# Moving one modulation vector from the value products to the first feed-forward block, with its steps ordered behind block products

## The chip, the cores and the metric

The kernel runs on one core of one Trainium2 chip, as one program. The core has a matrix engine (TensorE, PE in the profile, with its weight loads as PEld), VectorE (DVE), ScalarE (ACT), GpSimd (POOL) and a queue engine (SyncE, SP) that issues most of the transfers. Each engine works through its own list of instructions in order, and waits at the head of that list. The metric is the device time of one execution in microseconds (us), given as the median of several runs.

## The reference

Two layers of a diffusion backbone work on 512 latent and 256 context tokens of width 1024, all in float32. Every sub-layer normalises its input, scales and shifts it by a modulation vector, and adds its result to the stream through a gated post-norm. Layer 0 mixes tokens by gated linear attention and by softmax attention. Layer 1 mixes by a gated recurrence (HGRN2). Each is followed by a SwiGLU feed-forward block (FFN, 2816 hidden columns).

```python
m_lat = jnp.split((sc @ mod_w[l] + mod_b[l])[:, None, :], 6, axis=-1)
h_lat = _modulate(_rms(x_lat, norm_pre_mix[l]), m_lat[0], m_lat[1])
...
x_lat = x_lat + m_lat[2] * _rms(o_lat @ w_out, norm_post_mix[l])
h_lat = _modulate(_rms(x_lat, norm_pre_ffn[l]), m_lat[3], m_lat[4])
x_lat = x_lat + m_lat[5] * _rms(_swiglu(h_lat, ffn_w_gate[l], ffn_w_up[l], ffn_w_down[l]), norm_post_ffn[l])
```

There are thus six modulation vectors per layer, each a product of an activated condition (1024) with a block of `mod_w` of 1024 by 1024, 4 MB. The context tokens have six more from the same weights. In layer 1 the context is not needed behind the mixer, so only the vectors 0 and 1 are computed for it there. The text below writes (l, m) for vector m of layer l. The vector (1,4) scales the input of the second FFN; it is needed after layer 1's mixer.

## The kernel before

**Products.** Every float32 product is made as three products of split operands. ScalarE rounds an operand to its high part (wH, x, b11 and others), VectorE subtracts that to get the low part (wL and others), and `mm3` multiplies high by high, high by low and low by high. All matmuls are recorded at line 355 and all transposes at line 358, so tile names tell them apart.

**Modulation vectors.** `mod_late` (line 560) makes a vector without TensorE until its end. For each of eight blocks of 128 rows it loads 512 KB (line 578, on SP's queue) into a ring of two buffers (`mraw`), and VectorE multiplies the block by one number per partition and adds it to a sum (`macc`, lines 594 and 596). At the end TensorE adds the sum over the partitions (`mod_acc`), VectorE copies the row (line 469), TensorE transposes it (`modT`), and VectorE adds the bias (line 481). Where a gate follows, `gate_rows` (line 637) multiplies by a gain, transposes (`gcT`) and stores the row in HBM; `gate_row` (line 658) later loads it to all partitions as `gv`. `mod_late` is a generator: each call makes one step or a few, and hands back control. A call loads the next block before it sums the present one.

**The first FFN** (`ffn`, line 1544). `first` (line 1581) makes the first four columns of blocks and sums of the normalised input, split at line 98. Then for `idx` from 1 to 10 the gate and the up products are made by `seven` (line 839): seven block products in place of eight, each of 12 matmuls, into banks named a, E, b and D. VectorE and ScalarE add the banks to the outputs (lines 861 to 879) as each product ends. The weights come through `pair_operands` (line 801, with the splits of lines 798 and 799 and the sums of line 823). `seven` calls `fill` twice, behind its second and its fifth product, and `fill` calls the modulation generator `late` once. Before, `late` makes three jobs: (0,5) for both streams, (1,1) for both streams, and (1,5). `per=2` lets a job of one vector make two sums per call. At `idx` 9 whatever is left of `late` is issued at once, since its buffers are wanted.

**The down product** (`down`, line 1660) has seven passes over seven groups of blocks, with operands split at lines 1709 to 1712. Post-norms of finished tiles (`post_norm`, line 712; `pre_norm`, line 678) are generators in a list, and `tick` advances the earliest by one step. `turn` and `turn_next` issue the transposes of a tile (hT) whose normalised rows xn (line 685) are ready.

**The value products** stand at the end of the first FFN, in `values` (line 1997): the value columns of layer 1 for six tiles of tokens, in two halves c of 512 columns, with two tiles taken as a pair in each half. A tile and half has 24 matmuls (`nat`). Between tiles a generator `mods` makes vectors; before, its jobs are (1,2) together with (1,3), and then (1,4). The rest is drained when the products have been issued. Then `odd_mixer` (layer 1) begins with the products `ff` of its first head.

**What sets the order.** A planner puts each engine's instructions in a list before the run. It follows the order of the text where it must and takes ready work early where it may. While `self.pinned` is true, `pin` keeps TensorE's instructions in the order of the text; layer 1's mixer and the down products are pinned, the block products and, before, the value products are not. `tc.issue_after(ins)` makes every instruction issued inside it on `ins`'s engine follow `ins` in that engine's list; other engines and queues are not bound by it.

Of the kernel before, what the change touches and what calls it, by code (L numbers as in the profile page):

```python
# [8 lines left out]
F32 = mybir.dt.float32  # L9
# [4 lines left out]
ALU = mybir.AluOpType  # L14
# [50 lines left out]
class Forms:  # L65
# [29 lines left out]
    def split(self, n, f, i, m):  # L95
        H, L = (x[:, :, i : i + m] for x in self.tiles[n])
        self.net.nc.scalar.copy(H, f)
        self.net.nc.vector.tensor_tensor(L, f, H.bitcast(F32), op=ALU.subtract)

    def put(self, j, t):  # L100

# [215 lines left out]
class Net:  # L317
# [239 lines left out]
                yield  # L557
                rows()

    def mod_late(self, pool, jobs, tag="mraw", bufs=2, spare=None, per=1):  # L560


        nc = self.nc
        deep = bufs + (spare is not None) - 1
        for l, ms, then in jobs:
            self.mod_tiles(l, [m for m, r in ms if r == 0])
            accs = [pool.tile([P, D], F32, tag="macc", bufs=2, name=f"macc{l}{m}{r}") for m, r in ms]
            steps = [(k, m) for k in range(KD) for m in sorted({m for m, _ in ms})]
            us = []

            def load():
                i = len(us)
                k, m = steps[i]
                if spare is not None and i % (deep + 1) == deep:
                    u = spare()
                else:
                    u = self.wp.tile([P, WU], F32, tag=tag, bufs=bufs, name=f"mraw{l}{m}{k}")
                self.nc.sync.dma_start(out=u, in_=self.I["mod_w"][l, k * P : (k + 1) * P, m * D : (m + 1) * D])
                us.append(u)

            for _ in range(deep):
                load()
            yield
            done = 0
            for i, (k, m) in enumerate(steps):
                if len(us) < len(steps):
                    load()
                u, us[i] = us[i], None
                for a, (mm, r) in zip(accs, ms):
                    if mm != m:  # L590
                        continue
                    w = self.scT[:, k, r : r + 1]
                    if k == 0:
                        nc.vector.tensor_scalar(a, u, w, None, op0=ALU.mult)
                    else:
                        nc.vector.scalar_tensor_tensor(a, u, w, a, op0=ALU.mult, op1=ALU.add)  # L596
                    done += 1
                u = None
                if done % per == 0:
                    yield  # L600

            acc = self.tr_tile("mod_acc")
            for j in range(4):
                self.mm(
                    acc[32 * j : 32 * j + 32, :],
                    self.one.to_broadcast([P, 32]),
                    accs[(j // 2) % len(accs)][:, (j % 2) * 512 : (j % 2) * 512 + 512],
                    start=True,
                    stop=True,
                    tile_position=(0, 32 * j),  # L610
                )
            turned = self.mod_cols(l, acc, 512, [(m, r, 0, 2 * n, 0, 2) for n, (m, r) in enumerate(ms)])
            yield
            turned()
            if then:
                rows = self.gate_rows(l, *then)
                yield
                rows()
# [59 lines left out]
    def pre_norm(self, pool, t, xt, A, B, h):  # L678

        nc = self.nc  # L680
        r = 0 if t < LT else 1
        xn = pool.tile([P, D], F32, tag="xn", bufs=2, name=f"xn{t}")
        rs = self.rstd(self.sumsq(xt, xn), D)
        yield
        nc.vector.tensor_scalar(xn, xt, rs, None, op0=ALU.mult)
        tok = slice(t * P, (t + 1) * P)

        def turn():
            for hf in range(2):
                pt = self.tr_tile(f"hT{t}{hf}")  # L690
                forms = isinstance(h, Forms)
                f = h.at(hf, t) if forms else pool.tile([P, 4, P], F32, tag="hf", bufs=2, name=f"hf{t}{hf}")
                for kk in range(4):
                    k = hf * 4 + kk
                    self.tr(pt[:, kk * P : (kk + 1) * P], xn[:, k * P : (k + 1) * P], self.ident)
                for kk in range(4):
                    k = hf * 4 + kk
                    src = pt[:, kk * P : (kk + 1) * P]
                    nc.scalar.activation(f[:, kk, :], src, AF.Identity, bias=B[:, r, k : k + 1], scale=A[:, r, k : k + 1])
                if forms:  # L700
                    h.put(hf, t)
                else:
                    self.put(h, slice(hf * 4, hf * 4 + 4), tok, f)

        self.turns.append(turn)
# [133 lines left out]
    def seven(self, W, h, X, fill, then=None, turned=False):  # L839
# [4 lines left out]
        for wn, hn, x in SEVEN:  # L844
# [21 lines left out]
                        then()  # L866
                fill()
            elif wn == "12":
                nc.vector.tensor_tensor(c11, c11, pt, op=ALU.add)
            elif wn == "U2":  # L870
                nc.scalar.copy(c12, pt)
            elif wn == "22":
# [3 lines left out]
                nc.vector.tensor_tensor(c12, c12, pt, op=ALU.add)  # L876
            else:
                nc.vector.tensor_tensor(c21, c21, pt, op=ALU.subtract)
                nc.vector.scalar_tensor_tensor(c22, pt, -1.0, c22, op0=ALU.mult, op1=ALU.subtract)

    def rows_unit(self, w, c, pool=None):
        return self.unit(w[c * P : (c + 1) * P, :].rearrange("p (o n) -> p o n", o=1), 1, D, pool)
# [661 lines left out]
    def ffn(self, l, xp, yp, fp, pp, rp, h, ending, extra=None):  # L1544
# [5 lines left out]
        np_ = NFC // 2  # L1550
        self.blocks = I["ffn_w_down"][l].rearrange("(i k p) m -> k p i m", k=2, p=P)
        extra = extra or iter(())
        fill = lambda: next(extra, None)
        self.banks(True)
        qp = self.open_pool(f"q{l}", "right")
        qa = qp.tile([P, np_, 2, n], F32, name="qa")
# [60 lines left out]
        for idx in range(1, np_):  # L1617
            c0 = 2 * idx
            if qb[idx] is None:
                for _ in extra:  # L1620
                    pass
                qb[idx] = fp.tile([P, D], F32, tag="macc", bufs=2, name="qb")[:, : 2 * n].rearrange("p (a b) -> p a b", a=2)
            step = fill if idx > 1 else lambda: None
            last = []
            if idx == np_ - 1:
                down = self.down(l, fp, qp, rp, xp, quad, early, tiles, n, ending, lambda: todo())
# [33 lines left out]
    def down(self, l, fp, qp, rp, xp, quad, early, tiles, n, ending, finish):  # L1660
# [93 lines left out]
        for p, (name, where) in enumerate(seven):  # L1754
# [4 lines left out]
            for at, (g, i) in enumerate(order):  # L1759
# [43 lines left out]
                elif name == "22":  # L1803
                    plus(y1[:, low], b)
                    self.later(end(y1, t1))
                    self.tick()
                    if l and i == nh - 1:
                        close = final(dp, y0, t0)
                else:
# [8 lines left out]
    def run(self):  # L1818
# [162 lines left out]
        for _ in mods:  # L1981
            pass
        h1 = Split(ha)
        late = self.mod_late(
            fp, ((0, ((5, 0), (5, 1)), (5, R_NQF)), (1, ((1, 0), (1, 1)), None), (1, ((5, 0),), (5, R_NQF, 1))), per=2
        )

        def ending(dp):
# [8 lines left out]
            def values():  # L1997
# [1 line left out]
                self.tr_tile("pre"), self.sc_tile("pre", 0), self.sc_tile("pre", 1)  # L1999
                fi = yp.tile([P, len(order), D], F32, tag="y", bufs=1, name="fi")  # L2000
                spare = lambda: fp.tile([P, 2, 2 * forms.n], F32, tag="go", bufs=1, name="mraw").rearrange("p a n -> p (a n)")[:, :WU]
                mods = self.mod_late(fp, ((1, ((2, 0), (3, 0)), (2, R_NQM, 1)), (1, ((4, 0),), None)), spare=spare)
                for c in range(2):
                    pairs = [order[4:], order[:2]][c]
                    for t in order:
# [4 lines left out]
                        for i in range(4):  # L2010
                            W = value(c, i)
                            for a, x in enumerate(ts):
                                for k in (2 * i, 2 * i + 1):
# [4 lines left out]
                                        k == 0,  # L2018
                                        k == KD - 1,
                                    )  # L2020
                            if len(ts) > 1 and c == 0:
                                next(mods, None)
                                value(1, i)
                            if len(ts) > 1 and c == 1:
                                next(mods, None)
                        for a, x in enumerate(ts):
                            self.nc.scalar.copy(fi[:, x, 512 * c : 512 * c + 512], pt[:, 512 * a : 512 * a + 512])
                        if c == 0 and len(ts) == 1:
                            self.turn_next()
                            self.tick(5)  # L2030
                        if len(ts) == 1 and (c or t == order[3]):
                            for _ in range(4):
                                next(mods, None)
                for _ in mods:
                    pass
                ep.release()
# [109 lines left out]
```

## Time and profile before

| | |
|---|---|
| median of 3 runs | 1719.78 us (1719.2 to 1720.59) |
| the profiled execution | 1718.21 us, span 1716.3 us |
| busy: TensorE, weight loads | 1649.0 us, 1479.8 us |
| busy: VectorE, ScalarE, GpSimd | 1313.2 us, 929.7 us, 131.0 us |
| granted TensorE clock, mean | 0.991 |
| moved by DMA | 204.79 MB, mean 119 GB/s |

The stages around the change, from the timeline: the first FFN's entry from about 418 us, its block products from 457 to 754 us, its down product to 921 us, the value products to 999 us, then layer 1's mixer.

A row of the timeline gives start, length, engine, line, operation, output and inputs with their shapes, how often, and in brackets how long the engine sat idle before it and what ended that. A row of waits gives who waited for whom: total us, times, longest. A row of windows gives a stretch, its length, each engine's busy time with the count of instructions, the granted clock and the share of the DMA engines. A row of the chain gives start, length and what the chain that ended last was doing. Matmuls overlap, so starts tell more than lengths.

### The profile page before, as it was taken

What the parts mean: (1) busy time and instruction counts of PE and PEld (TensorE: products, weight loads), DVE (VectorE), ACT (ScalarE), POOL (GpSimd) and SP (SyncE); (2) the same over time, 40 slices, a digit from 0 to 9 for tenths busy, and PEclk for the clock granted to TensorE, in tenths of its full rate; (3) what the DMA queues carried; (4) which work ended last, traced back from release to release, by engine and by line L of the source; (5) the groups of instructions that cost most, each with busy time, mean ns of one, the idle gap of its engine ahead of it and who ended that gap; (6) DMA issues with size and microseconds to landing.
All of it is one profiled execution on the core that took longest, in us unless ns stands there. A gap on an engine that the chain in (4) does not pass through costs nothing.

```text
span 1716.3 us, 32583 instructions
## 1 busy us (share of the span) xinstructions
PE 1649.0 (96%) x13359; PEld 1479.8 (86%) x13359; DVE 1313.2 (77%) x2138; ACT 929.7 (54%) x1615; POOL 131.0 (8%) x135
## 2 busy tenths in 40 slices
PE   6999998999999999999998969999999999999997
PEld 5899987888999999998876758888988899999875
DVE  4889678875987898677667547878775489998887
ACT  4745568846544444445457316666564465555654
POOL 1004110011000000003101000000000000000221
PEclk9999999999999999999999979999999999999999
DMA  9641012175332435249426642112115333433793
GB/s 324 190 151 40 2 49 86 48 234 169 91 92 72 135 111 160 68 159 193 79 94 237 196 135 75 47 43 63 50 28 171 112 121 111 123 100 92 194 193 135
DMA packets 184961, 204.79 MB, mean 119 GB/s; under 512 B 7366, under 2 KB 142060, under 8 KB 184812
## 3 DMA queue, kind: packets, MB, share of 16 engines
q1 hardware_dynamic: 173760, 181.82, 33.7%
q0 software_dynamic: 9120, 17.30, 5.8%
q10 hardware_dynamic: 1932, 3.59, 0.6%
q8 instruction: 104, 1.70, 0.4%
q14 instruction: 45, 0.37, 0.1%
HBM read 193.23 MB, written 9.46 MB: 118 GB/s over the span
## 4 chain that ended last, share of the span: by engine, by line
PE 79%; DVE 8%; DMA 6%; ACT 4%; issue 2%; POOL 0%; SPq 0%; DVEq 0%; POOLq 0%; ACTq 0%
PE a L355 11%; PE nat L355 10%; PE ff L355 8%; PE x L355 8%; PE E L355 7%; PE oproj L355 5%; PE o L355 4%; PE D L355 4%; PE b L355 4%; DMA mraw<-in_mod_w_dram 3%; PE fq L355 3%; PE gqk L355 2%; PE q L355 2%; PE S L355 1%; PE poh L355 1%
## 5 line engine op out<-in xcount | busy, mean ns | idle before, releaser
L355 PE MATMUL nat<-wH,x 128*128 128x256 f32 (+2 forms) x992 | 232.8, 324 | 7.2 <-ACT x L709 3.3
L355 PEld LDWEIGHTS nat<-wH,x 128*128 128x128 f32 x992 | 167.3, 191 | 26.6 <-ACT x L709 4.8
L798 ACT CAST wH<-raw 128x1024 fp32r<-128x1024 f32 x120 | 125.5, 1051 | 107.2 <-PE b L355 29.8
L799 DVE TENSOR_TENSOR wL<-raw,wH 128x1024 fp32r<-128x1024 f32 x120 | 146.1, 1221 | 37.1 <-ACT wH L798 36.5
L355 PE MATMUL nat<-wL,x 128*128 128x256 f32 (+2 forms) x496 | 158.8, 320 | 0.4 <-DVE wL L744 0.3
L743 ACT CAST wH<-raw 128x1024 fp32r<-128x1024 f32 (+1 forms) x84 | 85.9, 1036 | 94.3 <-PE ff L355 34.1
L744 DVE TENSOR_TENSOR wL<-raw,wH 128x1024 fp32r<-128x1024 f32 (+1 forms) x84 | 99.9, 1199 | 48.1 <-ACT wH L743 47.3
L667 POOL TENSOR_TENSOR rs<-ms,neghalf 128x1 f32<-128x1 f32 (+2 forms) x62 | 69.9, 1131 | 861.0 <-DVE ms L665 860.8
L355 PE MATMUL ff<-x,wH 128*128 128x512 f32 (+1 forms) x512 | 129.7, 344 | 0.0
L355 PE MATMUL x<-wH,two 128*128 128x512 f32 x310 | 102.4, 397 | 5.2 <-DVE two L1712 3.3
L355 PE MATMUL oproj<-wH,x 128*128 128x512 f32 x320 | 102.2, 395 | 0.4 <-ACT x L1262 0.4
L355 PEld LDWEIGHTS nat<-wL,x 128*128 128x128 f32 x496 | 94.7, 191 | 7.0 <-DVE wL L744 1.0
L596 DVE SCALAR_TENSOR_TENSOR macc<-mraw,scT,macc 128x1024 f32<-128x1024 f32 x70 | 89.1, 1279 | 14.0 <-DMA mraw<-in_mod_w_dram 13.8
L355 PEld LDWEIGHTS ff<-x,wH 128*128 128x128 f32 x512 | 89.1, 194 | 10.0
L1677 POOL DMA_DIRECT2D t<-in_ffn_w_down_dram x42 | 45.0, 1149 | 647.9 <-DVE wL L1711 619.6
L950 ACT COPY qkh<-arr 128x512 f32<-128x512 f32 x112 | 70.0, 641 | 36.3 <-DVE arr L955 32.2
L355 PE MATMUL ff<-x,wL 128*128 128x256 f32 (+1 forms) x256 | 87.1, 340 | 0.0
L823 DVE TENSOR_TENSOR raw<-raw 128x512 f32<-128x512 f32 x120 | 82.6, 688 | 2.3
L355 PEld LDWEIGHTS x<-wH,two 128*128 128x128 f32 x310 | 58.0, 189 | 20.5 <-DVE two L1712 6.5
L955 DVE TENSOR_TENSOR arr<-arr,f 128x512 f32<-128x512 f32 x112 | 74.2, 687 | 1.9 <-ACT qkh L950 0.3
L355 PE MATMUL a<-T,wH 128*128 128x384 f32 (+1 forms) x320 | 70.7, 310 | 0.3 <-ACT qb L861 0.2
L355 PE MATMUL E<-x,wH 128*128 128x384 f32 (+1 forms) x320 | 70.7, 310 | 0.0
(413 smaller groups left out, 4528.5 us busy)
## 6 DMA issues: line engine op xcount, KB each, us to landing
mraw<-in_mod_w_dram SPq DMA_DIRECT2D x80, 512.0 KB, 4.6
raw<-in_ffn_w_gate_dram SPq DMA_DIRECT2D x44, 512.0 KB, 4.2
raw<-in_ffn_w_up_dram SPq DMA_DIRECT2D x44, 512.0 KB, 3.8
raw<-in_odd_w_in_dram SPq DMA_DIRECT2D x40, 512.0 KB, 3.7
t<-in_ffn_w_down_dram POOLq DMA_DIRECT2D x24, 512.0 KB, 7.9
raw<-in_ffn_w_down_dram SPq DMA_DIRECT2D x22, 512.0 KB, 5.0
mraw<-in_mod_w_dram SPq DMA_DIRECT2D x32, 256.0 KB, 6.1
raw<-in_even_w_in_dram SPq DMA_DIRECT2D x16, 512.0 KB, 4.8
```

The costliest lines, as they stand in the source:

```text
L355: return self.pin(self.nc.tensor.matmul(*a, **k))
L596: nc.vector.scalar_tensor_tensor(a, u, w, a, op0=ALU.mult, op1=ALU.add)
L667: nc.gpsimd.tensor_tensor(rs, ms, self.neghalf.to_broadcast([P, w]), op=ALU.pow)
L743: nc.scalar.copy(H[:, :m], raw[:, :m])
L744: nc.vector.tensor_tensor(L[:, :m], raw[:, :m], H[:, :m].bitcast(F32), op=ALU.subtract)
L798: self.nc.scalar.copy(H, f)
L799: self.nc.vector.tensor_tensor(L, f, H.bitcast(F32), op=ALU.subtract)
L823: add = lambda o, x, y: nc.vector.tensor_tensor(o, x, y, op=ALU.add)
L950: nc.scalar.copy(qkv[:, :, :, half, :], dst)
L955: nc.vector.tensor_tensor(dst, dst, tb, op=ALU.mult)
L1677: add = lambda o, src: self.pin(nc.gpsimd.dma_start(out=o, in_=src, accum_op=ALU.add))
```

## The change

1. `late` in the first FFN gets a fourth job, (1,4). A job with two sums per block still makes one block per call; a job of one vector now makes three sums per call, not two (`per` becomes a function of the number of sums).
2. `seven`, `pre_norm` and `Forms.split` record some of their VectorE instructions in `self.mark`. `fill` issues the modulation steps under `issue_after(self.mark)`, so on VectorE they come behind the last recorded instruction. `fill` is now also called at `idx` 1.
3. In the value products `mods` keeps only (1,2) with (1,3). Its calls go through `mod`, which uses `issue_after` too. They are spread as four behind the fourth single tile of the first half, one per quarter of the pairs, and two behind each single tile of the second half. `self.pinned` is true while the value products are issued.
4. In `down` the `tick` behind the sixth pass (`22`) is removed; it applied to both FFNs.

```diff
     def split(self, n, f, i, m):
...
-        self.net.nc.vector.tensor_tensor(L, f, H.bitcast(F32), op=ALU.subtract)
+        self.net.mark = self.net.nc.vector.tensor_tensor(L, f, H.bitcast(F32), op=ALU.subtract)
...
-    def mod_late(self, pool, jobs, tag="mraw", bufs=2, spare=None, per=1):
+    def mod_late(self, pool, jobs, tag="mraw", bufs=2, spare=None, per=lambda n: 1):
...
-                if done % per == 0:
+                if done % per(len(ms)) == 0:
                     yield
...
-        nc.vector.tensor_scalar(xn, xt, rs, None, op0=ALU.mult)
+        self.mark = nc.vector.tensor_scalar(xn, xt, rs, None, op0=ALU.mult)
...
-                nc.vector.tensor_tensor(c11, c11, pt, op=ALU.add)
+                self.mark = nc.vector.tensor_tensor(c11, c11, pt, op=ALU.add)
...
-                nc.vector.scalar_tensor_tensor(c22, pt, -1.0, c22, op0=ALU.mult, op1=ALU.subtract)
+                self.mark = nc.vector.scalar_tensor_tensor(c22, pt, -1.0, c22, op0=ALU.mult, op1=ALU.subtract)
...
-        fill = lambda: next(extra, None)
+        def fill():
+            with self.tc.issue_after(self.mark.ins):
+                next(extra, None)
...
-            step = fill if idx > 1 else lambda: None
+            step = fill
...
                     self.later(end(y1, t1))
-                    self.tick()
...
-            fp, ((0, ((5, 0), (5, 1)), (5, R_NQF)), (1, ((1, 0), (1, 1)), None), (1, ((5, 0),), (5, R_NQF, 1))), per=2
+            fp, ((0, ((5, 0), (5, 1)), (5, R_NQF)), (1, ((1, 0), (1, 1)), None), (1, ((5, 0),), (5, R_NQF, 1)), (1, ((4, 0),), None)),
+            per=lambda n: 2 if n > 1 else 3,
...
-                mods = self.mod_late(fp, ((1, ((2, 0), (3, 0)), (2, R_NQM, 1)), (1, ((4, 0),), None)), spare=spare)
+                mods = self.mod_late(fp, ((1, ((2, 0), (3, 0)), (2, R_NQM, 1)),), spare=spare)
+                self.pinned = True
+
+                def mod(n):
+                    with self.tc.issue_after(self.mark.ins):
+                        for _ in range(n):
+                            next(mods, None)
...
-                            if len(ts) > 1 and c == 0:
-                                next(mods, None)
-                                value(1, i)
-                            if len(ts) > 1 and c == 1:
-                                next(mods, None)
+                            if len(ts) > 1:
+                                mod(1)
+                                if c == 0:
+                                    value(1, i)
...
-                        if len(ts) == 1 and (c or t == order[3]):
-                            for _ in range(4):
-                                next(mods, None)
+                        if t == order[3] and c == 0:
+                            mod(4)
+                        elif c and len(ts) == 1:
+                            mod(2)
+                self.pinned = False
```

## The prediction

> **What bounds it.** I read the page first (span, engines, the chain by line), then the waits of TensorE by stretch, then the chain and the timeline where those waits lie.
>
> ```profile
> span 1716.3 us, 32583 instructions
> PE 1649.0 (96%) x13359; PEld 1479.8 (86%) x13359; DVE 1313.2 (77%) x2138; ACT 929.7 (54%) x1615; POOL 131.0 (8%) x135
> PE 79%; DVE 8%; DMA 6%; ACT 4%; issue 2%; POOL 0%; SPq 0%; DVEq 0%; POOLq 0%; ACTq 0%
> ```
>
> TensorE holds 79% of the chain and is busy for 96% of the span. A gain must therefore close a hole in TensorE's row; moving work between VectorE, ScalarE and the queues counts only where a hole opens or closes. The waits of TensorE, first from 405 to 457 us (entry of the first FFN), then from 755 to 1020 us (its down product, the value products, the entry of layer 1), show where the holes are:
>
> ```profile
> PE pearly L355 <- DVE x L98: 3.7, 1, 3.7
> ...
> PE mod_acc L355 <- DVE macc L596: 14.6, 1, 14.6
> PE x L355 <- DVE two L1712: 2.6, 2, 1.5
> PE nat L355 <- DVE x L710: 2.2, 1, 2.2
> ...
> PE nat L355 <- ACT wH L743: 1.3, 1, 1.3
> ```
>
> One wait of 14.6 us is far larger than the rest: TensorE stands before the column sum (mod_acc) of a modulation vector. The chain shows what it stands for; columns are start, length, what:
>
> ```profile
> 1013.75 1.97 PE mod_acc L355 x8
> ...
> 1016.49 1.12 PE modT L358 x4
> 1017.61 18.67 PE ff L355 x96
> ...
> 1041.72 2.88 PE ff L355 x24
> ...
> 1045.03 8.35 PE ff L355 x48
> ...
> 1055.52 5.68 PE ff L355 x24
> ```
>
> This is the last vector, (1,4): its eight blocks are loaded and summed when the value products are over, and the program puts its sum and transposes ahead of layer 1's first product (ff).
>
> **Part 1, vector (1,4) leaves the end of the value stage.** The last value product and the small transposes that now lie between the products:
>
> ```profile
> 986.41 1.06 PE L355 MATMUL mod_acc<-macc,one 128*32 128x512 f32 x8
> 988.44 0.60 PE L358 MATMUL modT<-ident,modrows 128*128 128x128 f32 x4
> 989.59 0.27 PE L358 MATMUL gcT<-ident,gc 128*8 128x128 f32 x1
> 998.78 0.39 PE L355 MATMUL nat<-wH,x 128*128 128x512 f32 x1
> ```
>
> The products end at 998.78 + 0.39 = 999.17 and ff begins at 1017.61 (chain): 18.44 us. With (1,4) gone, what stands there is the tail of the job that stays, (1,2) with (1,3). Its 20 calls end behind the last tile: the transposes (modT), VectorE's columns, then gcT. From the start of modT to the end of gcT they took 989.86 - 988.44 = 1.42 us. The TensorE work in it, about 0.6 us net of overlap, leaves the products, so the net price is 0.8 us. Gain 18.44 - 0.8 = 17.6 us.
>
> ff also runs faster. Its 96 matmuls took 18.67 us here and 2.88 + 8.35 + 5.68 = 16.91 us in the next head, 1.76 us less. The granted clock (the figure behind the POOL column) says why:
>
> ```profile
> 912.47:916.00 3.53, 3.53 (x9) 2.80 (x10) 3.11 (x5) 1.88 (x4) 0.24 (x1) 0.55 0.88 309
> 440.16:443.00 2.84, 2.84 (x16) 2.84 (x17) 2.84 (x4) 1.24 (x2) 0.00 (x0) 1.00 0.02 6
> 1013.75:1017.26 3.51, 2.70 (x12) 0.97 (x13) 0.70 (x2) 0.00 (x0) 0.00 (x0) 0.50 0.02 6
> 1017.26:1021.90 4.64, 4.64 (x24) 4.64 (x23) 0.33 (x2) 0.00 (x0) 0.00 (x0) 0.50 0.00 0
> ```
>
> After the long wait the clock is half for 8.1 us, 4.64 of them inside ff. So 1.8 us more goes, 19.4 in all. [...] The rows disagree: 8.1 us slow here, 0.55 after a wait of at most 1.5 us (912.47), and 1.00 after the 3.7 us wait (440.16). [...]
>
> What is late next: ff needs its first weight splits, which today are held between the vector's steps on VectorE; without those steps they follow the release of the last four weight slots, while the last tile's products still run. Cover here is some 4 us of products; if it failed, each split (1.2 us) would show once.
>
> **Part 2, (1,4) enters the first FFN.** Eight loads of 512 KB, eight VectorE steps, one column sum, four transposes and a column add go between the block products (columns behind the window: busy time of PE, PEld, DVE, ACT, POOL, then clock, DMA share, GB/s; the fourth and fifth row count the instructions on macc alone):
>
> ```profile
> 498.60:542.30 43.70, 43.70 (x254) 43.70 (x253) 28.94 (x41) 19.82 (x29) 0.00 (x0) 1.00 0.25 73
> 574.10:624.50 50.40, 50.40 (x292) 50.31 (x291) 50.16 (x63) 20.35 (x31) 0.00 (x0) 1.00 0.49 145
> 643.00:672.00 29.00, 28.89 (x169) 28.54 (x168) 25.36 (x34) 11.54 (x17) 0.00 (x0) 1.00 0.64 199
> ...
> 574.10:624.50 50.40, 0.00 (x0) 0.00 (x0) 19.36 (x16) 1.00 0.49 145
> 643.00:672.00 29.00, 0.00 (x0) 0.00 (x0) 9.72 (x8) 1.00 0.64 199
> ...
> 616.87 4.16 PE a L355 x24
> 631.43 4.16 PE a L355 x24
> ...
> 677.15 4.16 PE a L355 x24
> ```
>
> A set of seven products lasts 631.43 - 616.87 = 14.56 us. Without steps VectorE is busy 28.94 of 43.70 us, so 4.9 us per set are free. From set 1 of index 1 to the end of index 8 there are 16 sets, 79 us free, against 48 steps at about 1.2 us (19.36 / 16, 9.72 / 8) = 58 us: it fits, at some 91% load. The row from 574 to 624 is the hardest case seen: 16 steps, VectorE busy throughout, TensorE without a hole. The loads bring 4.2 MB more; at a DMA share of 0.64 (643 to 672) TensorE lost 0.11 us. The four jobs need 31 calls (11, 10, 5, 4 and one to end); indices 1 to 8 make 32, so the drain at index 9 finds nothing.
>
> Price of one more vector: the sets from 631.43 to 677.15 took 45.72 against 3 x 14.56 = 43.68; 2.04 us cover one column sum, its transposes and all stalls of the single vector summed there. I take 2.0. Bounds: 1.7 (1.06 + 0.60) and 10, the latter if the three chained steps per call hold VectorE (rival 1).
>
> **Part 3, steps queued behind block products (the marks).** A step may not be placed on VectorE before the last marked instruction. At the entry of the first FFN this bites:
>
> ```profile
> 425.00:437.20 12.20, 0.00 (x0) 0.00 (x0) 7.77 (x7) 1.00 0.58 184
> ...
> 439.42 0.68 DVE L98 TENSOR_TENSOR x<-f,x 128x512 fp32r<-128x512 f32 x1
> ...
> 438.39 0.61 ACT L97 CAST x<-f 128x512 fp32r<-128x512 f32 x1
> ```
>
> The first row is VectorE's work on macc between 425 and 437.2 us: seven steps, ahead of the split (L98, 439.42) for which TensorE waits 3.7 us. The first call's mark is the last split of the entry, so all seven go behind it. Then the ScalarE cast, now at 438.39 behind a cast that waits for a VectorE sum, can follow its inputs at once, about 3 us earlier. Gain 3.3; bounds 0 (something else holds the cast) and 3.7. The steps displaced are in part 2's 48. Their loads sit in two buffers until the steps free them, and SP's queue behind them holds weight loads; three weight buffers hold one set and a half.
>
> **Part 4, one post-norm start later (the removed tick).** In both FFNs the first post-norm step of a tile is now issued among the last block's operands, not before them.
>
> ```profile
> 890.30 1.23 DVE L720 TENSOR_TENSOR pn<-y,gv 128x1024 f32<-128x1024 f32 x1 [1.70 <-DMA gv<-gd]
> 893.10 0.73 PE L355 MATMUL x<-wH,two 128*128 128x512 f32 x2 [1.48 <-DVE two L1712]
> 1688.71 0.69 DVE L2074 TENSOR_TENSOR pl<-y,gv 128x512 f32<-128x512 f32 x1 [2.72 <-DMA gv<-gd]
> ```
>
> In the first FFN, pn holds VectorE 1.70 us for the gate row, and TensorE waits 1.48 us for the operand behind it. I take a gain of 1.5; bounds 2.6 (both waits for two above) and a loss of 2, if the later post-norm makes the next transposes late. In the second FFN another instruction (L2074), whose place in the text stays, waits for the same row: 0.3 gained, within 1 either way.
>
> **Part 5, value products pinned.** Transposes can no longer slip between the products of the first tile, where the weight wait of 1.3 us stands; they then cost their time behind it. VectorE's first steps move behind the last xn (L685, 941.43) from 937.96, some 4 us:
>
> ```profile
> 937.96 0.76 DVE L594 TENSOR_SCALAR macc<-mraw,scT 128x1024 f32<-128x1024 f32 x1 [1.55 <-DMA mraw<-in_mod_w_dram]
> ...
> 941.43 0.78 DVE L685 TENSOR_SCALAR xn<-xr,rs 128x1024 f32<-128x1024 f32 x1 [0.73 <-POOL rs L667]
> ...
> 970.93 1.28 DVE L596 SCALAR_TENSOR_TENSOR macc<-mraw,scT,macc 128x1024 f32<-128x1024 f32 x1 [0.51 <-DMA mraw<-in_mod_w_dram]
> ```
>
> The last step would end near 976; the sum is now called behind the last tile but one, near 993, so 17 us cover it. I take a loss of 1.0; bounds: gain 2.2 (the wait for x L710 goes) and loss 4.
>
> **Sum.** -19.4 + 2.0 - 3.3 - 1.5 - 0.3 + 1.0 = -21.5 us. The profiled execution took 1718.2 us; the median is 1.6 above it. 1719.8 - 21.5 = 1698.3, say 1698.
>
> **Rivals.** 1, slower: the single vectors now take three steps per call with two buffers, so the third step must wait for a load that starts when the first ends. If VectorE stands there with the next evacuation behind it, TensorE stops.
>
> ```profile
> mraw<-in_mod_w_dram SPq DMA_DIRECT2D x80, 512.0 KB, 4.6
> ```
>
> Six such groups (3, 3 and 2 steps, twice) at 4.6 us, each with up to 1.6 us of half clock (the nine matmuls of 912.47 took 3.53), cost 37 us: 1735. It decides from 21.5 / 6 = 3.6 us a group. Against it: eight chained steps in 29.00 us left TensorE 28.89 busy.
>
> 2: the marks change nothing at the entry, since the cast is late for another reason: 1701.6.
>
> 3: the pinned order exposes waits at tile changes, the upper bound of part 5 and one slow restart: +3.0 + 1.6, 1703.
>
> 4: ff is slow for another reason than the wait before it and keeps its 18.67 us: 1700. [...]
>
> **Chances.** Forecast (1693 to 1701) 0.54; rivals 2 and 3, 0.14 each; rival 4, 0.06, since the clock rows speak against it; rival 1, 0.12, of which 0.09 end slower and 0.03 close to today. A measurement of this kernel tells about 0.2% (3.4 us) from no change: faster 0.88, same 0.03, slower 0.09. The range runs from 1691 (the gain bounds of parts 2 to 5 together, 5.7 us below 1698.3, less the 1.4 us that the runs spread) to 1707 (rivals 2 and 3 together).
>
> **What would show it.** Part 1: no wait of mod_acc for macc before ff, under 2 us between the last value product and ff, the clock near 1.00 in ff. Part 2: a fourth column sum among the block products, their stretch 1.7 to 2.5 us longer. Part 3: no macc step ahead of the entry's splits and no wait of pearly for x. Part 4: two and wL ahead of pn. Part 5: no transposes inside the first value tile. The forecast fails if VectorE's steps wait for mraw in the block products while TensorE waits for E or wL, or if mod_acc waits again inside the value stage.

## The result and the profile after

The changed kernel takes 1706.78 us, the median of four runs (1705.05 to 1708.56); before took 1719.94 us in the same comparison. The ratio is 0.9924, with a 95% interval from 0.9907 to 0.9941: 13.2 us faster. The forecast was 1698, range 1691 to 1707. The sign and the main mechanism were right; the time lies at the upper edge of the range, because 5.3 us of the difference stand at a step to which I had given a gain. That it still lies inside, by 0.2 us, is luck: the upper end was rivals 2 and 3 together, and neither is what cost the time.

The head of the page of the profile after, with the chain by engine (the profiled execution took 1708.56 us, the longest of the four):

```profile
span 1706.8 us, 32587 instructions
PE 1649.5 (97%) x13359; PEld 1481.9 (87%) x13359; DVE 1313.8 (77%) x2138; ACT 930.3 (55%) x1615; POOL 126.8 (7%) x135
PE 81%; DVE 8%; DMA 4%; ACT 4%; issue 2%; POOL 1%; DVEq 0%; SPq 0%; POOLq 0%; ACTq 0%
```

TensorE's busy time did not move (1649.0 before), nor did VectorE's. What went is waiting: the share of DMA in the chain fell from 6% to 4%. The chain around the place that mattered most:

```profile
1000.59 4.32 PE nat L355 x18
...
1007.53 0.14 issue
1007.66 0.27 PE gcT L358
1007.93 16.68 PE ff L355 x96
```

Where 18.44 us stood between the last value product and ff by the chain, 1.7 us stand now (the last product is at 1005.86 and lasts 0.40), and ff takes 16.68 us in place of 18.67. New waits of TensorE have come up, though. The first row below is from the block products (455 to 765 us), the next three from the down and value products (905 to 1012), the last from the second FFN's down product (1590 to 1712):

```profile
PE mod_acc L355 <- DVE macc L596: 3.0, 2, 1.5
...
PE nat L355 <- ACT wH L743: 3.0, 1, 3.0
PE nat L355 <- DVE x L710: 3.0, 1, 3.0
...
PE gcT L358 <- DVE gc L643: 1.0, 1, 1.0
...
PE x L355 <- DVE two L1716: 3.1, 2, 2.4
```

The table measures the stages on TensorE's timeline, from the first matmul of one stage to the first of the next, in us: *entry* from pearly to the first a, *blocks* to the first down product, *down 1* to the first value product, *values* to the end of the last one, *gap* to ff, *layer 1* to the second FFN's down product, *down 2* to the end of the span. Columns e1 to e9 are experiments told below; B and C (e10 and e11) are further profiles of the kernel before. By the starts and ends of the matmuls themselves a gap comes out some 0.3 us shorter than by the chain; matmuls overlap, so it can come out just below nothing.

| stage | before | B | C | after | e1 | e5 | e7 | e8 | e9 |
|---|---|---|---|---|---|---|---|---|---|
| up to pearly | 417.7 | 419.8 | 419.6 | 419.3 | 417.8 | 419.0 | 419.4 | 417.3 | 417.8 |
| entry | 39.1 | 41.7 | 42.0 | 35.1 | 35.1 | 35.1 | 35.1 | 35.1 | 35.1 |
| blocks | 296.9 | 297.1 | 298.1 | 301.3 | 300.8 | 298.2 | 301.7 | 298.5 | 298.3 |
| down 1 | 167.1 | 167.2 | 167.1 | 167.5 | 166.7 | 166.5 | 166.5 | 166.6 | 164.9 |
| values | 78.4 | 78.9 | 78.4 | 83.1 | 80.9 | 81.1 | 76.1 | 76.5 | 75.0 |
| gap | 18.1 | 17.6 | 17.7 | 1.4 | 1.4 | 1.4 | 1.4 | -0.1 | -0.1 |
| layer 1 | 579.0 | 577.8 | 577.0 | 576.9 | 576.8 | 577.5 | 576.7 | 576.6 | 576.5 |
| down 2 | 120.0 | 121.7 | 120.6 | 122.2 | 121.1 | 120.3 | 120.5 | 120.9 | 120.0 |
| span | 1716.3 | 1721.7 | 1720.4 | 1706.8 | 1700.6 | 1699.1 | 1697.4 | 1691.5 | 1687.6 |

The first row shows how far executions differ ahead of any edit: 2.5 us. Against the first profile of before the change gave: entry -4.0, gap -16.7, layer 1 -2.1, and lost blocks +4.4, values +4.6, down 2 +2.2. Against B and C some of these are other sizes (down 2 only +0.5 and +1.6, layer 1 -0.9 and -0.1); the last section shows where the profiles differ.

### The profile page after: what moved, and what is told of

Read it like the earlier page. It is cut to its first block, busy times and chain, and to the rows that moved or that the text cites. A ratio compares the mean times of both kernels' runs of the same rounds, so it can differ in the third digit from the quotient of the medians.

```text
span 1706.8 us, 32587 instructions
## 1 busy us (share of the span) xinstructions
PE 1649.5 (97%) x13359; PEld 1481.9 (87%) x13359; DVE 1313.8 (77%) x2138; ACT 930.3 (55%) x1615; POOL 126.8 (7%) x135
## 4 chain that ended last, share of the span: by engine, by line
PE 81%; DVE 8%; DMA 4%; ACT 4%; issue 2%; POOL 1%; DVEq 0%; SPq 0%; POOLq 0%; ACTq 0%
PE nat L355 11%; PE a L355 10%; PE ff L355 8%; PE x L355 8%; PE E L355 7%; PE oproj L355 5%; PE o L355 4%; PE D L355 4%; PE b L355 3%; PE fq L355 3%; DMA mraw<-in_mod_w_dram 2%; PE gqk L355 2%; PE pearly L355 2%; PE q L355 2%; PE S L355 2%
## 5 line engine op out<-in xcount | busy, mean ns | idle before, releaser
L667 POOL TENSOR_TENSOR rs<-ms,neghalf 128x1 f32<-128x1 f32 (+2 forms) x62 | 65.7, 1063 | 852.9 <-DVE ms L665 852.7
L355 PE MATMUL b<-x,wH 128*128 128x384 f32 (+1 forms) x320 | 70.7, 310 | 0.0
```

The lines of the kernel that those rows point to most:

```text
L355: return self.pin(self.nc.tensor.matmul(*a, **k))
L667: nc.gpsimd.tensor_tensor(rs, ms, self.neghalf.to_broadcast([P, w]), op=ALU.pow)
```

## The experiments

**Theory and rivals.** After the result the theory was: the vector's move and the marks gain what was forecast; the loss in the value stage and in both down products comes from the removed tick, which makes VectorE's post-norms late; and the blocks lose by a column sum that stands waiting for its last step. The rivals: the pinned order causes the loss in the values; the vector alone explains everything; the entry would have gained without the marks.

**e1: the tick put back** into the kernel after.

```diff
                 elif name == "22":
                     plus(y1[:, low], b)
                     self.later(end(y1, t1))
+                    self.tick()
```

> The changed kernel with the removed tick put back. Theory A (without the tick, two post-norm products stand ahead of an operand split on VectorE in the second FFN's down product, and TensorE waits 2.4 us for it): that down product falls from 122.1 us to about 120, the first FFN's moves by less than 1 us, 1704.5 in all. Rival B (the 2.2 us there are spread between executions or a reshuffle by the planner that has nothing to do with the tick): within 0.5 us of the changed kernel, the 2.4 us wait stays.

Measured 1703.27 us (1702.67 to 1703.93), ratio to before 0.9904 [0.9891, 0.9917]. Theory A: 3.5 us of the loss are the tick. The two intervals overlap a little, so the stages decide: values 83.1 to 80.9, down 2 from 122.2 to 121.1, down 1 from 167.5 to 166.7. VectorE in the second FFN shows how; first the kernel after, then e1 (start, length, line, operation):

```profile
1682.27 1.22 DVE L720 TENSOR_TENSOR pn<-y,gv 128x1024 f32<-128x1024 f32 x1
1683.41 0.14 DVE L665 TENSOR_SCALAR ms<-sq 128x1 f32<-128x1 f32 x1
1683.47 1.21 DVE L1715 TENSOR_TENSOR wL<-raw,wH 128x1024 fp32r<-128x1024 f32 x1
1685.14 1.28 DVE L729 SCALAR_TENSOR_TENSOR xr<-pn,rs,xr 128x1024 f32<-128x1024 f32 x1 [0.46 <-POOL rs L667]
1686.35 1.22 DVE L720 TENSOR_TENSOR pn<-y,gv 128x1024 f32<-128x1024 f32 x1
1687.48 0.68 DVE L1716 TENSOR_TENSOR two<-qb,two 128x512 fp32r<-128x512 f32 x1
...
1688.22 0.73 PE L355 MATMUL x<-wH,two 128*128 128x512 f32 x2 [2.41 <-DVE two L1716]
```

```profile
1680.69 1.22 DVE L720 TENSOR_TENSOR pn<-y,gv 128x1024 f32<-128x1024 f32 x1
1681.82 0.15 DVE L665 TENSOR_SCALAR ms<-sq 128x1 f32<-128x1 f32 x1
1681.88 1.22 DVE L1715 TENSOR_TENSOR wL<-raw,wH 128x1024 fp32r<-128x1024 f32 x1
1683.02 0.68 DVE L1716 TENSOR_TENSOR two<-qb,two 128x512 fp32r<-128x512 f32 x1
...
1683.15 0.50 PE L355 MATMUL x<-wL,two 128*128 128x512 f32 x1 [1.24 <-DVE wL L1715]
```

The post-norm is a chain: pn, a mean square (ms), GpSimd's root (rs), then xr. Without the tick it starts one call later, and its second half, the step xr with its 0.46 us wait for GpSimd and the next pn, comes to lie between wL and two: TensorE waits 2.41 us for two. With the tick that half falls elsewhere and TensorE waits 1.24 us, for wL. The larger loss, in the values, goes with the wait for wH: it is 3.0 us in the three kernels without the tick (after, e2, e6) and 1.3 us in the ten other profiles. The kernel after and e6 also run at half clock near the start of the values (0.50 from 928.27 to 935.10 us in the kernel after; in e6 eight transposes take 1.91 us at 932.14, where e1's take 1.04), and once more in down 2 (1689.44 to 1692.86 us; in e6 128x512 matmuls of 0.63 us from 1706.43, where the next, from 1709.93, take 0.40). How a step of VectorE's makes that cast of ScalarE's late was not followed.

**e2: the value products not pinned**, the rest as after.

```diff
-                self.pinned = True
                 def mod(n):
...
-                self.pinned = False
```

> The changed kernel with the value products not pinned. Theory A (the pinned order exposes waits in the value stage): the wait of 3.0 us for wH in the first tile falls towards 1.3 us as before, the stage shortens by 2 to 4 us, 1703 to 1705. Rival B (those waits come from the weight casts' place on ScalarE and from the sums' place on VectorE, which pinning does not set): less than 0.7 us of difference, the waits stay where they are.

Measured 1707.18 us (1703.81 to 1709.98), ratio 0.9927 [0.9915, 0.9939]: theory A fell; nothing changes. The values take 83.4 us, and the wait for wH stands there as in the kernel after, 3.0 us. One wait does go, 1.2 us for wL, but the wait for x grows from 3.0 to 3.3 us. The pin did not cause the loss here; e9 comes back to it.

**e3: the vector alone** in the kernel before.

```diff
-            fp, ((0, ((5, 0), (5, 1)), (5, R_NQF)), (1, ((1, 0), (1, 1)), None), (1, ((5, 0),), (5, R_NQF, 1))), per=2
+            fp, ((0, ((5, 0), (5, 1)), (5, R_NQF)), (1, ((1, 0), (1, 1)), None), (1, ((5, 0),), (5, R_NQF, 1)), (1, ((4, 0),), None)), per=2
...
-                mods = self.mod_late(fp, ((1, ((2, 0), (3, 0)), (2, R_NQM, 1)), (1, ((4, 0),), None)), spare=spare)
+                mods = self.mod_late(fp, ((1, ((2, 0), (3, 0)), (2, R_NQM, 1)),), spare=spare)
```

> The kernel before with only the vector (1,4) moved to the first FFN (two sums per call, no marks, no pinning, the tick kept). Theory A (the move itself is worth what was forecast, 19.4 less 2.0, and the rest of the change eats part of it): 1719.9 - 17.4 = 1702.5, faster than the whole change. Rival B (the shortfall belongs to the move: the steps in the first FFN and the value stage without its last vector cost more than read): 1706 or more.

Measured 1706.03 us (1702.2 to 1709.02), ratio 0.9921 [0.9907, 0.9935]. One edit of the four gives what all four give together; the other three cancel. It is less than A's 1702.5 because the 28 calls at indices 2 to 8 are too few for four jobs with two sums a call, so the rest is issued at once at index 9, and the blocks grow by 7.9 us. TensorE there, and the stretch from 700 to 730 us (columns: PE, PEld, DVE, ACT, POOL busy, clock, DMA share, GB/s):

```profile
723.61 1.93 PE L355 MATMUL mod_acc<-macc,one 128*32 128x512 f32 x8 [3.31 <-DVE macc L596]
...
700.00:730.00 30.00, 26.69 (x143) 24.64 (x142) 23.61 (x31) 10.39 (x16) 0.00 (x0) 0.89 0.54 170
```

The values take 78.8 us in it and the entry 39.1, as before. So the longer value stage does not come with the vector's move.

**e4: the marks alone** in the kernel before.

```diff
-        self.net.nc.vector.tensor_tensor(L, f, H.bitcast(F32), op=ALU.subtract)
+        self.net.mark = self.net.nc.vector.tensor_tensor(L, f, H.bitcast(F32), op=ALU.subtract)
...
-        fill = lambda: next(extra, None)
+        def fill():
+            with self.tc.issue_after(self.mark.ins):
+                next(extra, None)
```

> The kernel before with only the marks in the block products (fill under issue_after), nothing moved. Theory A (the steps behind the marks free the entry of the first FFN and cost nothing in the products): the 3.7 us wait for x goes, 1716 in all. Rival B (steps behind the marks push the sums and TensorE's column sums late, so the products lose what the entry gains): 1719 to 1721, with waits of mod_acc for macc in the block products.

Measured 1712.07 us (1710.3 to 1715.67), ratio 0.9958 [0.9946, 0.997]: 7.9 us, twice what theory A had (1716). The entry is 35.1 us, as in the kernel after, and no wait of pearly is left in its block products. That is 4.0 us against the first profile of before; e10 and e11 show up to 2.9 us more. Its down 1 takes 165.0 us where the three profiles of before have 167.1 to 167.2, but no edit lies in that stage: all three of before run at half clock near its end (0.50 from 912.84 to 916.25 us in the first; a 128x512 matmul takes 0.63 us in place of 0.39 from 918.75 in B and from 919.74 in C), this profile does not (0.39 there, from 895 us to the first value product at 914.10).

**e6: the tick alone** taken out of the kernel before.

```diff
                     plus(y1[:, low], b)
                     self.later(end(y1, t1))
-                    self.tick()
```

> The kernel before with nothing changed but the tick of the down product taken away. Theory A (the tick's removal costs by itself, because VectorE's next-tile work is queued a product later): the second FFN's down stage goes from 120.0 to 121 to 122 and the value stage from 78.4 to 80 to 81; about 1723.5 against 1720. Theory B (it costs only beside the vector in the first FFN and the marks, whose steps then stand in the way): within 1 us of 1720. The forecast's own sum for this edit was a gain of 1.8.

Measured 1726.71 us (1725.98 to 1731.12) against 1719.33, ratio 1.0045 [1.0029, 1.0062]. It costs 7.4 us by itself, twice theory A. Its values take 80.7 us, its two down products 168.5 and 122.5 (78.4, 167.1 and 120.6 in C): together 5.6 us against C. So three single edits, -14.0 (e3), -7.9 (e4) and +7.4 (e6), add up to -14.5; the change gave -13.2.

**e10, e11: the kernel before, profiled again** (B and C in the table). No edit.

> The kernel before, unchanged, profiled in another execution. In the first profile TensorE waited 3.7 us at the entry of the first FFN and went on at a granted clock of 1.00; in the profile of the kernel before without its tick it waited 3.4 us there and went on at 0.50 until 446.4. Theory A (the clock after such a wait is a matter of the execution, so the marks, which remove the wait, save 2 us more than the first profile shows): half clock here in some of the profiles, entry stage 41 us instead of 39. Theory B (the missing tick made that difference): clock 1.00 and 39.1 us.

> The same again, a third profile of the kernel before: entry stage 39.1 us with the clock at 1.00 after the wait, or about 41.3 us with the clock at 0.50 for 5 us.

Single executions of 1723.66 and 1722.22 us. Theory A: TensorE waits at the entry as in the first profile, but goes on at half clock in both. The row of the wait in e11, then the clock behind it (columns: PE busy, clock, DMA share, GB/s) in e11, in the kernel before without its tick (e6), and in e3, which kept 1.00:

```profile
442.32 0.69 PE L355 MATMUL pearly<-x,wH 128*128 128x384 f32 x1 [3.98 <-DVE x L98]
...
442.32:447.00 4.68, 4.68 (x15) 0.50 0.02 4
```

```profile
441.23:446.00 4.77, 4.77 (x15) 0.50 0.02 3
```

```profile
441.19:446.00 4.81, 4.81 (x27) 1.00 0.01 3
```

In about the same time 27 matmuls run at full clock and 15 at half. Of five profiles with this wait, three show half clock behind it (3.44, 3.98, 4.07 us) and two do not (3.67, 3.69 us). So the entry costs 41.3 to 42.0 us in some executions and 39.1 in others, and the marks are worth 4.0 to 6.9 us: I had read one execution of the cheaper kind. What decides between the two is not shown by any run (last section).

**e5: the column sum one product later**, on top of e1.

```diff
+            if len(ms) == 1:
+                yield
             acc = self.tr_tile("mod_acc")
```

> The kernel after with the removed tick put back and, for a single vector, one more yield between the last step on VectorE and TensorE's column sum, so that one more product stands between them. Theory A (the 4.4 us that the block products grew by are mostly a column sum that reaches TensorE 1.5 us before VectorE's last step): TensorE's wait for macc at mod_acc falls from 2.5 to 3.0 us to under 0.5, the block stage from 300.8 to about 298.5, and the time from 1703.3 to about 1701. Theory B (the stage is longer by the four columns' own matmuls and transposes and by slower products beside the steps): the wait goes and the stage stays within 0.8 of 300.8; 1703 or more.

Measured 1698.99 us (1697.59 to 1701.2), ratio 0.9879 [0.9861, 0.9896]. Theory A: the blocks go from 300.8 to 298.2 us, and TensorE has no wait left in them. In the kernel after the last step of a vector starts only 1.4 us before its sum:

```profile
639.59 1.28 DVE L596 SCALAR_TENSOR_TENSOR macc<-mraw,scT,macc 128x1024 f32<-128x1024 f32 x1
...
641.02 1.06 PE L355 MATMUL mod_acc<-macc,one 128*32 128x512 f32 x8 [1.50 <-DVE macc L596]
```

With three steps a call and no call between, the sum stands directly behind the last steps in the text, and TensorE comes to it 1.5 us early, twice. The median fell by 4.3 against e1, the stage by 2.7; the two were not measured on the same chip, and the rest is within what executions differ.

**e7: the modulation steps behind the splits of x as well**, on top of e1.

```diff
-        self.nc.vector.tensor_tensor(L, f, H.bitcast(F32), op=ALU.subtract)
+        self.mark = self.nc.vector.tensor_tensor(L, f, H.bitcast(F32), op=ALU.subtract)
```

> The kernel after with the removed tick put back and the modulation steps put behind the last split of x as well (the mark is set there too). Theory A (steps that begin behind the last normalisation stand in front of the split of x in VectorE's order and wait there for a transfer, so that TensorE's first products of the next tile wait 3 us): the wait for x goes from 3 us to under 1, the value stage from 80.9 to about 78 and the time from 1703.3 to about 1700. Theory B (the steps are pushed towards the end of the stage, and the last column sum waits for them): the wait for x goes, a wait for macc of 2 us or more stands at the end of the stage, and the time stays within 1 of 1703.3.

Measured 1698.64 us (1697.68 to 1699.98), ratio 0.9876 [0.9859, 0.9892]. Theory A: the values go from 80.9 to 76.1 us. VectorE and TensorE of the kernel after around the wait that e7 removes:

```profile
959.48 1.28 DVE L596 SCALAR_TENSOR_TENSOR macc<-mraw,scT,macc 128x1024 f32<-128x1024 f32 x1 [0.95 <-DMA mraw<-in_mod_w_dram]
960.68 0.68 DVE L710 TENSOR_TENSOR x<-hf,x 128x512 fp32r<-128x512 f32 x1
...
961.42 0.73 PE L355 MATMUL nat<-wH,x 128*128 128x512 f32 x2 [2.99 <-DVE x L710]
```

Behind the last xn VectorE takes modulation steps and splits of x in turns. A step that waits 0.95 us for its load holds the split behind it, and TensorE waits for that split. In e7 the last split is at 956.48 and the first step at 957.09; the steps then end at 991.7 us, and no product waits for them.

**e8: all three mends together**, with one of the modulation calls moved from a tile change to the inside of the last tile:

```diff
+                            elif c and t == order[5] and i == 1:
+                                mod(1)
...
-                            mod(2)
+                            mod(1 if t == order[5] else 2)
```

> The tick put back, the later column sum, the steps behind the splits, and one modulation call moved from the value stage's tile changes to the inside of its last tile, together on top of the kernel after. If the three losses are separate places on TensorE's path they add up: blocks 298.5, values about 78, down 121, in all about 1697 to 1699. If VectorE only passes its lateness on to the next place, the time is no better than the best of the single edits, 1700 or more.

Measured 1695.28 us (1693.96 to 1697.0), ratio 0.9856 [0.984, 0.9873]. The losses were separate places and their removal adds up: blocks 298.5, values 76.5. The last call's place takes the gap of 1.4 us too: gcT's wait for gc now falls behind products.

**e9: e8 with the values not pinned**, the edit of e2.

> The three mends together, with the value products free in order again (not pinned). Theory A (the order that the scheduler finds for the value products is the source's order or as good, so the pin is worth nothing either way): within 1.5 us of 1695.3, value stage within 1 us of 76.6. Theory B (the pin's price was hidden under the late splits and shows now that they are gone, as the forecast's +1.0 had it): faster by 1 us or more, value stage below 75.6; or it protects the order and its loss costs 2 or more.

Measured 1693.27 us (1689.39 to 1693.6) against 1720.48, ratio 0.9837 [0.9823, 0.9852]; the best kernel of the study. The interval overlaps e8's, but the waits of TensorE from 900 to 1012 us say what went. First e8, then e9:

```profile
PE nat L355 <- DVE wL L746: 2.3, 2, 1.5
PE nat L355 <- ACT wH L745: 1.3, 1, 1.3
```

```profile
PE nat L355 <- ACT wH L745: 1.3, 1, 1.3
...
PE nat L355 <- DVE wL L746: 0.2, 1, 0.2
```

Unpinned, the transposes of the next tile come forward into these waits; e9's timeline has six of them there, where e8 has none until its first tile is done:

```profile
918.96 0.51 PE L355 MATMUL nat<-wH,x 128*128 128x512 f32 x1 [1.26 <-ACT wH L745]
919.30 0.82 PE L358 MATMUL hT<-ident,xn 128*128 128x128 f32 x6
```

```profile
924.91 0.50 PE L355 MATMUL nat<-wL,x 128*128 128x512 f32 x1 [1.54 <-DVE wL L746]
...
927.53 1.03 PE L358 MATMUL hT<-ident,xn 128*128 128x128 f32 x8
```

That is the pin's price, 2.0 us at the medians, 1.5 in the value stage. The two profiles differ by 3.9 us, but 1.7 of that is not the pin: in down 1, with nearly the same waits, e8 runs at half clock for a while (mean 0.99 from 760 to 915 us, matmuls of 0.63 us in place of 0.39 from 910.14 to 912.27) and e9 does not (1.00). In the kernel after the price did not show (e2): the wait for the late splits of x grew by 0.3 us, which may have taken back some of what the transposes gained; where the rest went no run shows.

## Why the prediction was right or wrong

**Part 1 (forecast -19.4): right.** The gap fell by 16.2 to 16.7 us, by the profile of before one compares with, and ff by 2.0 or 0.8, since in B and C it took 17.52 and 17.49 us: -18.7 with the first profile, -17.0 and -17.1 with B and C. The clock in ff is 1.00 (from 1012 to 1025), so rival 4 is out: the slow stretch went with the wait. How far that stretch reached into ff was a matter of the execution, to 1022.07 in the first profile, some 4.5 us, and 1.8 us in B and C (mean clock 0.56 and 0.51 from 1020 to 1025). The 8.1 us that I read were the end of a longer stretch: in the first profile the clock is half from 1001.59, early in the wait, to 1022.07. Why the rows beside it read 0.55 behind a wait of at most 1.5 us and 1.00 behind one of 3.67 us no run shows (last section). The tail costs 1.4, not 0.8 net: the first weight splits of ff do run beside the last products, as I said, but one of them (1006.02, 1.22 us, in the rows of the chain below) stands on VectorE ahead of the columns, and gcT waits 1.0 us for those. e8 shows that the tail need cost nothing.

```profile
1004.93 1.07 ACT wH L743
...
1006.02 1.22 DVE wL L744
1007.24 0.15 DVE modcol L481 x2
1007.39 0.14 DVE gc L643
```

**Part 2 (+2.0, bounds 1.7 and 10): the term was too small by 1.2 to 2.4.** A fourth column sum stands among the blocks, as forecast; they measured +4.4 against the first profile, +4.2 and +3.2 against B and C. I priced the single vector from a set in which one was summed; that row had two sums per call. With three the column sum comes sooner behind the last step, and TensorE waits 1.5 us twice (e5). Of rival 1 that is all there is: no chained step waited long enough for its load to stop TensorE anywhere else in the blocks.

**Part 3 (-3.3, bounds 0 and 3.7): the mechanism right, the size too small.** No step stands ahead of the entry's splits in the kernel after, and pearly waits for nothing. The gain is 4.0 against the first profile of before, 6.6 against B and 6.9 against C. The step that failed is the clock: I took the 1.00 behind 440.16 as the rule for such a wait and left the half clock out of the bound; B, C and e6 have 0.50 behind waits of 4.07, 3.98 and 3.44 us.

**Part 4 (-1.8, bounds -2.6 and +2 in the first FFN): the wrong sign; the step of the forecast that failed.** I argued that the post-norm, which holds VectorE for the gate row, would come behind the operands. In the kernel after it stays where it was:

```profile
891.82 1.23 DVE L720 TENSOR_TENSOR pn<-y,gv 128x1024 f32<-128x1024 f32 x1 [1.21 <-DMA gv<-gd]
```

It still stands ahead of two and wL (893.55 and 894.42), in the kernel after as in e1 (889.90 there, with 1.28 us of waiting for gv); what came a call later was what stands behind it in the list (ms, 896.43, where e1 has it at 891.04). The change therefore lost 3.5 us here (e1) in place of gaining 1.8, and 7.4 in the kernel before (e6). My bound of a loss "if the later post-norm makes the next transposes late" named the mechanism, but only for the first FFN, and a tick moves each later step of the list in both.

**Part 5 (+1.0, bounds -2.2 and +4): within the bounds, for other reasons.** The pin costs 1.5 to 2.0 us where nothing hides it (e9) and shows no price in the kernel after (e2). The steps did move behind the last xn (949 to 982 us; I had 976), and the column sum is covered, as I said. What I missed is that there they meet the splits of x, behind the same xn: the wait for x was 2.2 us and became 3.0, where I had it as a possible gain. Queued behind the splits too, they cost nothing (e7, -4.9 in the values).

**The sum.** Forecast -21.5, measured -13.2 by the medians. Against the first profile the misses are +0.7 (part 1), +2.4 (part 2), -0.7 (part 3), +5.3 (part 4: from -1.8 to +3.5), and what is left of the values, some 1.5 (4.6 longer, less 2.1 of the tick and the 1.0 of the forecast): 9.2. Against C they are +2.3, +1.2, -3.6, +5.3 and 1.5: 6.7. To be explained is 8.3. Rival 3's time, 1703, came nearer than the forecast's, but its mechanism, the pinned order, was not what cost the time here (e2).

## What to carry to other kernels

On an engine where a waiting step holds what stands behind it, as on VectorE here (a step waited 0.95 us for its load, and TensorE 2.99 us for the split behind it), place work that waits for a transfer behind everything that another engine is about to need, not only behind some of it: the marks paid at the entry and cost in the value stage for want of one more mark (e7). Before removing a step from a paced list, follow all that comes behind it in that list: the step itself may not move at all. Profile the kernel before more than once if a stall of 3 to 4 us on TensorE is in the sum, since the clock behind it differed between executions here: 1.00 in the first profile of before, 0.50 in B and C.

## What the runs showed that was not expected

The granted clock behind a wait does not follow from the wait's length alone. Half clock came after waits of 3.44 (e6), 3.98 (C) and 4.07 us (B) at the entry and full clock after 3.67 (the first profile) and 3.69 us (e3) at the same place; in the kernel after it was half after 1.76 us (915.13) and after 2.99 us (929.10), as these two stretches show (columns: PE busy, clock, DMA share, GB/s):

```profile
915.13:918.00 2.87, 2.87 (x7) 0.50 1.03 380
929.10:934.00 4.90, 3.74 (x8) 0.50 0.64 188
```

In the first profile of before the clock is half from 912.84 to 916.25, from 953.80 to 957.21 and from 1001.59 to 1022.07 us; in the kernel after from 914.62 to 918.03, from 928.27 to 935.10 and from 962.40 to 965.82. It turned while TensorE still waited at 914.62 and 928.27, ahead of the matmuls at 915.13 and 929.10, and in C at 441.20, ahead of the one at 442.32. The entry in C around that point, then in the first profile of before, which kept 1.00, in stretches as long (same columns):

```profile
437.79:441.20 3.41, 0.55 (x4) 1.00 0.52 154
441.20:444.61 3.41, 2.29 (x7) 0.50 0.02 5
...
434.97:438.39 3.42, 1.52 (x9) 1.00 0.51 141
438.39:441.80 3.41, 1.64 (x9) 1.00 0.08 28
441.80:445.21 3.41, 3.41 (x22) 1.00 0.00 0
```

In C TensorE was busy for 0.55 us of the 3.41 ahead of the turn. In the first profile the two stretches that share the wait hold 1.52 and 1.64 us of work, around 3.67 us without any, and the clock stayed. Short waits came before a turn too: from 911.20 to the turn at 914.62 in the kernel after, one wait of 1.06 us and most of the next, of 1.76 us, leave TensorE busy for 1.10 us of 3.42. The ends of matmuls are modelled, so the busy times are rough. That it matters where a wait lies in time, beside its length, was my reading of these stretches; no run shows it. After the long wait in the first profile the clock came back only at 1022.07, behind 4.46 us of ff through which TensorE was busy.

Executions of the same program part by up to 2.5 us before the first edit is reached (417.3 to 419.8 us in the table), though TensorE's instructions up to there come in the same order (4404 records, tile by tile, in the first profile and in the kernel after). The profiles whose mean clock over the first 330 us is 1.00 (the first profile, e8, e9) reach pearly at 417.3 to 417.8 us, those with 0.99 (B, C, the kernel after) at 419.3 to 419.8; in the kernel after the clock is half from 262.67 to 266.08. The difference is as much as the pin, the column sum's wait or the tail are worth: these could be told only by stages.
